# Nearest-neighbour upsampling: the input in two blocks of 61 and 451 rows per partition

## The chip, the core and the metric

The kernel runs on one core of one Trainium2 chip. The metric is the device time of one execution in microseconds; comparisons use the median of several runs.

## The reference

```python
batch, channels, h, w = x.shape          # 16, 64, 64, 64, float32
new_h, new_w = (h * scale_factor, w * scale_factor)      # scale_factor = 2
for i in range(new_h):
    for j in range(new_w):
        result[:, :, i, j] = x[:, :, i // scale_factor, j // scale_factor]
```

Each input row of 64 values becomes two equal output rows of 128 values, each value standing twice. The input has 16.78 MB, the output 67.11 MB.

## The kernel before

The input is seen as 65,536 rows of 64 floats (256 B). Partition p of 128 gets the 512 rows from 512 p on; their output is one stretch of 512 KB in HBM, 1 KB per input row. Everything lives in one SBUF tile, `mem`: ahead of the input area (`xt`, R = 512 rows) lies a free area of 79 output rows' size (`FREE`, `WF`).

Three loads, all issued by SP at L197, bring 32, 256 and 224 rows of each partition (`HEAD`, `cuts`). They are moved ahead of the program's opening barrier by `begin_before_barrier`.

Then nine steps follow, of the row counts in `rows`. In each, VectorE copies k input rows of every partition into an output buffer of k x 256 floats, reading each value twice and each row twice (`expanded`, L217; the first step's first row has a copy of its own at L216). Then one DMA stores the buffer (L219). Buffers alternate: even steps write at the front of the tile, odd steps just below the end of the input that has been consumed so far, so that the buffer grows into spent input. A step's copy therefore waits for the store two steps back, while the store one step back is under way. SP issues the stores of steps 0, 1 and 8, ACT the other six:

```python
rows = [54, 38, 54, 60, 54, 62, 64, 62, 64]
k0 = 1 if n == 0 else 0
issuer = nc.sync if n in (0, 1, len(rows) - 1) else nc.scalar
```

`close_early` rearranges the program's end so that only the last store's semaphore is waited for on SP after the closing barrier. Neither it nor `begin_before_barrier` is touched.

Of the kernel before, what the change touches and what calls it, by code (L numbers as in the profile page):

```python
# [153 lines left out]
@with_exitstack  # L154
def kernel(
    ctx: ExitStack,
    tc: tile.TileContext,
    x: bass.AP,
    scale_factor: int,
    out: bass.AP,  # L160
):
    nc = tc.nc
    nc.at_finalize(begin_before_barrier)
    nc.at_finalize(close_early)
    P = nc.NUM_PARTITIONS
    s = int(scale_factor)
    B, C, H, W = x.shape
    R = B * C * H // P
    fdt = x.dtype

    xp = x.rearrange("b c h w -> (b c h) w").rearrange("(p r) w -> p r w", p=P)
    op = out.rearrange("b c (h hd) w -> (b c h) (hd w)", hd=s).rearrange(
        "(p r) w -> p r w", p=P
    )

    rows = [54, 38, 54, 60, 54, 62, 64, 62, 64]
    GROW = s * s
    FREE = 79
    WF = FREE * GROW * W
    assert sum(rows) == R
    mem_pool = ctx.enter_context(tc.tile_pool(name="mem", bufs=1))
    LEAD = 32
    whole = mem_pool.tile([P, LEAD + WF + R * W], fdt, name="mem")
    mem = whole[:, LEAD:]
    xt = mem[:, WF:].rearrange("p (r w) -> p r w", r=R)  # L190

    HEAD = 32
    cuts = [0, HEAD, R // 2 + HEAD, R]
    for lo, hi in zip(cuts, cuts[1:]):
        nc.sync.dma_start(out=xt[:, lo:hi], in_=xp[:, lo:hi])  # L197

    def expanded(r0, r1):
        return (  # L200
            xt[:, r0:r1].unsqueeze(2).unsqueeze(4).to_broadcast([P, r1 - r0, s, W, s])
        )

    r0 = 0
    before = (0, 0)
    for n, k in enumerate(rows):
        size = k * GROW * W
        at = 0 if n % 2 == 0 else WF + r0 * W - size
        assert at >= before[1] or at + size <= before[0]
        before = (at, at + size)  # L210
        u = mem[:, at : at + size].rearrange(
            "p (k a w b) -> p k a w b", k=k, a=s, w=W
        )
        k0 = 1 if n == 0 else 0
        if k0:
            nc.vector.tensor_copy(out=u[:, :k0], in_=expanded(r0, r0 + k0))  # L216
        nc.vector.tensor_copy(out=u[:, k0:], in_=expanded(r0 + k0, r0 + k))  # L217
        issuer = nc.sync if n in (0, 1, len(rows) - 1) else nc.scalar
        issuer.dma_start(out=op[:, r0 : r0 + k, :], in_=u)  # L219
        r0 += k  # L220


# [33 lines left out]
```

## Time and profile before

| what | value |
|---|---|
| median of 3 runs | 197.28 us (197.05 to 197.37) |
| profiled execution, its own time | 197.08 us |
| its span, first to last instruction | 195.8 us |
| VectorE busy | 76.9 us in 10 copies |
| moved by DMA | 83.89 MB in 12 transfers, 1728 packets |
| mean rate over the span | 429 GB/s |

The span is what the profile shows; the time also holds what lies around it. A packet is one piece of a transfer on one of 16 DMA engines. "DMA" rows in the profile give the mean busy share of the 16 engines, "GB/s" what they moved, the bytes of a packet being booked as a whole, so that slices of a few microseconds scatter around the true rate.

### The profile page before, as it was taken

Reading aid. Unit: us, or ns where it says so; the run is one execution under the profiler, and the core shown is the slowest. Engines: PE = TensorE matmul, PEld = TensorE weight load, DVE = VectorE, ACT = ScalarE, POOL = GpSimd, SP = SyncE. Lnnn points to the kernel's source line nnn. Section 1 sums busy time; section 2 is a strip of 40 time slices with the busy share of each in tenths; the row PEclk is TensorE's granted clock in tenths of the full one; section 3 lists DMA queues with packets and bytes.
Section 4 is the critical chain, followed back from the end, with each engine's and each line's share of the span. In section 5 each row is a group of like instructions: output and inputs, shape, how many; then the busy total and the mean of one; then the engine's idle time right before and its main releaser. Section 6 shows DMA issues by size and latency. Waiting matters only on the chain.

```text
span 195.8 us, 76 instructions
## 1 busy us (share of the span) xinstructions
DVE 76.9 (39%) x10; POOL 0.2 (0%) x4
## 2 busy tenths in 40 slices
DVE  0000099990029287059008805920790079000000
POOL 0000000000000000000000000000000000000000
DMA  9999989989898988999999899999999999999994
GB/s 429 429 429 429 402 375 539 398 362 542 362 435 382 551 373 362 542 402 402 402 537 407 362 542 415 415 415 415 429 429 429 429 415 558 473 435 422 429 429 214
DMA packets 1728, 83.89 MB, mean 429 GB/s; under 512 B 192, under 2 KB 192, under 8 KB 192
## 3 DMA queue, kind: packets, MB, share of 16 engines
q10 hardware_dynamic: 864, 46.66, 55.0%
q1 hardware_dynamic: 864, 37.22, 44.2%
HBM read 16.78 MB, written 67.11 MB: 429 GB/s over the span
## 4 chain that ended last, share of the span: by engine, by line
DMA 61%; DVE 24%; SPq 0%; issue 0%
DMA out_dram<-mem 49%; DVE mem L217 24%; DMA mem<-in_x_dram 12%; SPq L197 0%
## 5 line engine op out<-in xcount | busy, mean ns | idle before, releaser
L217 DVE COPY mem<-mem 128x13824 f32<-128x13824 f32 (+5 forms) x9 | 76.6, 8515 | 84.6 <-DMA out_dram<-mem 65.6
L216 DVE COPY mem<-mem 128x256 f32<-128x256 f32 x1 | 0.3, 293 | 4.8 <-DMA mem<-in_x_dram 4.8
L237 POOL MEMSET const-bfloat16-1.0<- 128x1 bf16 x1 | 0.1, 102 | 0.0
L237 POOL MEMSET const-uint8-127<- 128x1 uint8 x1 | 0.1, 101 | 0.0
L237 POOL MEMSET const-float32-0.0<- 128x1 f32 x1 | 0.1, 98 | 0.2 <-issue 0.2
L237 POOL MEMSET const-float32-1.0<- 128x1 f32 x1 | 0.1, 98 | 0.0
## 6 DMA issues: line engine op xcount, KB each, us to landing
out_dram<-mem ACTq DMA_DIRECT2D x2, 7936.0 KB, 31.6
out_dram<-mem ACTq DMA_DIRECT2D x2, 6912.0 KB, 23.7
out_dram<-mem ACTq DMA_DIRECT2D x1, 7680.0 KB, 26.1
mem<-in_x_dram SPq DMA_DIRECT2D x1, 7168.0 KB, 40.2
out_dram<-mem SPq DMA_DIRECT2D x1, 6912.0 KB, 19.0
out_dram<-mem SPq DMA_DIRECT2D x1, 4864.0 KB, 25.2
mem<-in_x_dram SPq DMA_DIRECT2D x1, 1024.0 KB, 4.8
mem<-in_x_dram SPq DMA_DIRECT2D x1, 23.7
```

The costliest lines, as they stand in the source:

```text
L216: nc.vector.tensor_copy(out=u[:, :k0], in_=expanded(r0, r0 + k0))
L217: nc.vector.tensor_copy(out=u[:, k0:], in_=expanded(r0 + k0, r0 + k))
L237: nc = _bacc.Bacc("TRN2", target_bir_lowering=False, num_devices=1)
```

## The change

The rows of the input are cut into two blocks. Block A is the first 128 x 61 rows, 61 to a partition: in HBM it is one unbroken stretch, and so is its output. Block B is the rest, 451 rows to a partition. A is loaded first, in one DMA, into the last 61 rows of the SBUF input area; B follows in two loads of 227 and 224 rows. The steps go through B first and end with A as one step of 61 rows. The row counts of steps 5 to 8 become 64, 64, 63 and 61, and every step with an odd count gets a one-row copy ahead of an even one.

```diff
-    xp = x.rearrange("b c h w -> (b c h) w").rearrange("(p r) w -> p r w", p=P)
-    op = out.rearrange("b c (h hd) w -> (b c h) (hd w)", hd=s).rearrange(
-        "(p r) w -> p r w", p=P
-    )
-    rows = [54, 38, 54, 60, 54, 62, 64, 62, 64]
+    A = 61
+    N = P * A
+    xr = x.rearrange("b c h w -> (b c h) w")
+    outr = out.rearrange("b c (h hd) w -> (b c h) (hd w)", hd=s)
+    xa = xr[:N].rearrange("(p r) w -> p r w", p=P)
+    xb = xr[N:].rearrange("(p r) w -> p r w", p=P)
+    oa = outr[:N].rearrange("(p r) w -> p r w", p=P)
+    ob = outr[N:].rearrange("(p r) w -> p r w", p=P)
+    rows = [54, 38, 54, 60, 54, 64, 64, 63, A]
...
-    HEAD = 32
-    cuts = [0, HEAD, R // 2 + HEAD, R]
-    for lo, hi in zip(cuts, cuts[1:]):
-        nc.sync.dma_start(out=xt[:, lo:hi], in_=xp[:, lo:hi])
+    B0 = R - A
+    CUT = 227
+    nc.sync.dma_start(out=xt[:, B0:], in_=xa)
+    nc.sync.dma_start(out=xt[:, :CUT], in_=xb[:, :CUT])
+    nc.sync.dma_start(out=xt[:, CUT:B0], in_=xb[:, CUT:])
...
-        k0 = 1 if n == 0 else 0
+        k0 = 1 if n == 0 or k % 2 else 0
...
-        issuer.dma_start(out=op[:, r0 : r0 + k, :], in_=u)
+        dst = ob[:, r0 : r0 + k, :] if n < len(rows) - 1 else oa
+        issuer.dma_start(out=dst, in_=u)
```

## The prediction

> **What bounds the kernel now.** I read the page first: parts 1 to 3 for what is busy, then the chain, then the trace by windows and the DVE timeline.
>
> ```profile
> DVE 76.9 (39%) x10; POOL 0.2 (0%) x4
> ...
> DMA  9999989989898988999999899999999999999994
> ...
> DMA packets 1728, 83.89 MB, mean 429 GB/s; under 512 B 192, under 2 KB 192, under 8 KB 192
> ...
> HBM read 16.78 MB, written 67.11 MB: 429 GB/s over the span
> ```
>
> VectorE works for 76.9 of 195.8 us, while the 16 DMA engines are full in every slice but the last. The 192 packets under 512 B are the completions of 12 transfers on 16 engines; the other 1536 are one run per partition per transfer. So the time is 83.89 MB through 16 engines, plus whatever the engines lose at the two ends. The windows, cut by hand at the start and the end, show those losses.
>
> ```profile
> 0.00:1.00 1.00, 0.00 (x0) 0.20 (x4) 1.00 0.00 0
> 1.00:2.40 1.40, 0.00 (x0) 0.00 (x0) 1.00 0.97 252
> ...
> 40.00:190.00 150.00, 60.78 (x8) 0.00 (x0) 1.00 1.00 433
> 190.00:194.90 4.90, 0.00 (x0) 0.00 (x0) 1.00 0.99 428
> 194.90:195.80 0.90, 0.00 (x0) 0.00 (x0) 1.00 0.01 0
> ```
>
> The last two columns are the share of the DMA engines in use and GB/s. In the long middle the share is 1.00 at 433 GB/s. The sum of the span: 83.89 MB / 433 GB/s = 193.7 us; nothing moves in the first 1.0 us; from 1.0 to 2.4 us the engines are called busy (0.97) but move 252 instead of 433 GB/s, which loses 1.4 x (1 - 252/433) = 0.6 us. That makes 195.3, and the last 0.5 of 195.8 is the uneven finish of the engines and the last completions. Outside the span lie 1.3 us, since this execution took 197.08. The median of the three runs is 197.28, so the profiled run is 0.2 us on the low side; I work out a difference and put it on the median.
>
> So a change can gain only from the 1.0 + 0.6 + 0.5 us at the ends, unless it alters the 433. It can lose anywhere that a queue runs empty. The chain of waits must be read with that in mind:
>
> ```profile
> 0.43 23.65 DMA mem<-in_x_dram
> 24.09 0.02 issue
> 24.11 14.30 DVE mem L217
> 38.41 0.02 issue
> 38.42 19.01 DMA out_dram<-mem
> 57.44 0.02 issue
> 57.46 7.37 DVE mem L217
> 64.83 0.02 issue
> ```
>
> It gives 24% to DVE, but those are stretches with other transfers in flight beside them; the windows show no dip under them. The copies matter only if one of them outlasts the transfers queued ahead of its store.
>
> **The change part by part.**
>
> First, DMA work. Rows read and written are the same (61 + 451 = 512 per partition), and so are the three loads, the nine stores and the 128 runs in each. The first load doubles nearly, from 32 to 61 rows; the second shrinks from 256 to 227, so that both together are still 288 rows; the third stays at 224. Bytes and packets don't change: 0 us in the middle, if the rate holds at 433.
>
> Second, the addresses in HBM. Partitions of the input stand 512 x 256 B = 128 KiB apart before and 451 x 256 B = 112.75 KiB after; of the output 512 KiB before and 451 KiB after. Block A is one unbroken stretch: 61 rows next to 61 rows. No row shows the new distances. Loads and stores at the two old distances are alike. The load issues are
>
> ```profile
> L197 SPq DMA_DIRECT2D mem<-in_x_dram x3: 382/425/432, 0.0 to 0.9; - x3
> ...
> mem<-in_x_dram SPq DMA_DIRECT2D x1, 7168.0 KB, 40.2
> ```
>
> so the third load, issued at 0.9, landed near 41.1; 16.78 MB less the 0.35 MB of the ramp (252 GB/s for 1.4 us) from 2.4 to 41.1 is 425 GB/s, and 429 if the last 0.4 us is completion. Stores alone follow at 433. A fourfold distance makes no difference over about 1%, so I take 0 for the middle, with bounds of 1% to both sides (a rival each, below).
>
> The Trainium skill (DMA: Bandwidth & Descriptors, "Latency and other measured facts") has a row against large powers of two as row pitch: at 512 KiB 207 GB/s per direction, at a padded pitch 214. By that ratio the stores alone, 67.11 MB, would take some 5 us less after the change. The trace speaks against it: the stores at just that pitch run at 433 GB/s. The same page ("Where 436 GB/s comes from") puts the ceiling at 435 GB/s, by which the middle has under 1 us to give at any pitch; this speaks against the change, and the 433 agrees with it.
>
> Third, the ramp. The 0.6 us between 1.0 and 2.4 us is lost while 16 engines begin to read 8 KB runs from rows that stand 128 KiB apart. If it is address collision, the unbroken block removes it; if it is the time to the first data of any load, nothing changes. Bounds: -0.6 (all of it goes) and +0.3 (runs of 15.25 KB double the part of the ramp in which engines hold each other up, half of 0.6). No row tells the two apart. I take -0.15, a quarter of the loss, nearer to none since some latency must stay.
>
> Fourth, the first store. Before, the one-row copy of L216 ran while the second load was under way; now it waits for the second load, whose data it reads, and stands ahead of the 53-row copy.
>
> ```profile
> 4.83 0.29 DVE L216 COPY mem<-mem 128x256 f32<-128x256 f32 x1 [4.83 <-DMA mem<-in_x_dram]
> 24.11 19.55 DVE L217 COPY mem<-mem 128x13568 f32<-128x13568 f32 x2 [18.99 <-DMA mem<-in_x_dram]
> 38.42 5.60 SPq L219 DMA_DIRECT2D out_dram<-mem  x2
> ```
>
> 24.11 is the landing of 288 rows and stays. The 0.29 us (0.31 with the gap) moves onto the way to the first store: it is issued at 38.73 instead of 38.42. What hides it is the third load, landing at 41.1, its data over by perhaps 40.7. The first load needed 1.0 us from issue to data, so the store's data can flow from 39.7: hidden, and I take 0. If a store needs the whole ramp of the first load, 2.4 us, it is at full rate at 41.1, after the load's end: up to 0.4 us then. Both ends stay for the range. Queued behind that store on SP are only the second store and the last one; on DVE behind the one-row copy all others, none of them short of cover.
>
> Fifth, the other copies. The 63- and 61-row steps get a one-row copy ahead of an even one.
>
> ```profile
> L217 DVE COPY mem<-mem 128x16384 f32<-128x16384 f32 x2 | 17.4, 8694 | 18.6 <-DMA out_dram<-mem 18.6
> L217 DVE COPY mem<-mem 128x15872 f32<-128x15872 f32 x2 | 16.9, 8427 | 21.0 <-DMA out_dram<-mem 21.0
> L217 DVE COPY mem<-mem 128x13568 f32<-128x13568 f32 x1 | 14.3, 14286 | 19.0 <-DMA mem<-in_x_dram 19.0
> L217 DVE COPY mem<-mem 128x15360 f32<-128x15360 f32 x1 | 8.2, 8161 | 4.2 <-DMA out_dram<-mem 4.2
> ```
>
> The 53-row row shows why: an odd count cost 14.3 us where 54 to 64 rows cost 7.4 to 8.7. With the split, 63 rows cost 0.29 + 8.43 = 8.7 and 61 rows 0.29 + 8.16 = 8.5 us. Each copy waits for the store two back and is covered by the store one back, k rows of which take k x 131 KB / 433 GB/s = 0.303 k us: 19.4 us for 64 rows, 19.1 for 63. A margin of 10 us: 0. The thinnest later margin, the 4.2 us of the 60-row copy's wait after the 54-row one, sits in steps that don't change.
>
> Sixth, the last store: 61 rows instead of 64, one unbroken stretch, on the same SP queue, beside a 63-row store on ACT instead of a 62-row one. The end depends on the total per engine, which is the same. The 0.9 us of the last window without new data stays: 0, by at most 0.1 us either way.
>
> Sum: 0 - 0.15 + 0 + 0 + 0 = -0.15 us; the profiled execution would go from 197.08 to 196.9, the median from 197.28 to 197.1.
>
> **The rivals.** 0.2% of 197.28 is 0.4 us, about what a measurement of this kernel can tell from no change.
>
> *The ramp was collision* and goes, almost whole: -0.4 to -0.6, 196.7 to 196.9. For it speaks that engines were busy 0.97 at 252 GB/s; against it that the second and third load have the same distances and show no such loss. 0.18.
>
> *The power-of-two distance costs something all along.* If the 433 is held down by 1%, the bound from the load against the store rate, the stores gain 1.5 us: 195.8. Against it: a share of 1.00 at one steady rate, loads and stores alike. 0.04.
>
> *The first store comes late (slower).* Its place is the join of loads and stores near 41 us: issue at 38.73, and a queue that is dry from 40.7. It decides if a store takes over 2.0 us from issue to full rate; the price is up to 0.4 us, and with a ramp that is no better (or 0.1 to 0.3 worse) 197.7 to 198.0. Against it: the 1.0 us to first data, and descriptors that wait in the queue while the load drains. 0.12.
>
> *The new distances are the worse ones (slower).* At every second partition, loads now start on odd multiples of 256 B and stores on odd multiples of 1 KiB. A rate lower by 1% costs 1.9 us: 199.2. Against it: runs of 38 to 64 KB, for which a row's first bytes hardly count. 0.08.
>
> *The change does nothing to the ramp* is within the forecast.
>
> **How the numbers follow.** The forecast, within 0.4 us of 197.28 and likeliest 197.1, has 0.58. Faster: 0.18 + 0.04 = 0.22; slower: 0.12 + 0.08 = 0.20. The range takes in the vanished ramp below (197.28 - 0.6 = 196.7, less 0.1 for the end: 196.6) and the late first store above (197.28 + 0.4 = 197.7); outside are the two cases of another rate, 0.12, and half of 0.12 for a late store on top of a worse ramp.
>
> **What would show it.** The windows of the changed kernel: again 433 GB/s from 40 to 190 us (or another rate: the distances matter); 1.0 to 2.4 us above 252 GB/s if the ramp was collision, the same if it was latency. The one-row copy at 24.1, the first store at 38.7, and near 41 us a DMA share without a dip. DVE at some 77 us of busy time in 12 copies, none of over 9 us but the 53-row one. The forecast is wrong if the span leaves 195.4 to 196.2 us.

## The result and the profile after

| kernel | median of 8 runs | range |
|---|---|---|
| before | 197.25 us | 197.05 to 197.55 |
| changed | 197.83 us | 197.56 to 198.10 |

The ratio is 1.0028 (95% interval 1.0017 to 1.0039): slower by 0.6 us. The profiled execution took 197.56 us with a span of 196.2; before it was 197.08 and 195.8. So the changed kernel's profile shows 0.4 to 0.5 us of the loss.

The first three windows and the middle of the changed kernel, with the same cuts as before (share of the DMA engines and GB/s in the last two columns):

```profile
0.00:1.00 1.00, 0.00 (x0) 0.20 (x4) 1.00 0.00 0
1.00:2.40 1.40, 0.00 (x0) 0.00 (x0) 1.00 1.14 245
2.40:4.00 1.60, 0.00 (x0) 0.00 (x0) 1.00 0.89 381
...
40.00:190.00 150.00, 61.69 (x10) 0.00 (x0) 1.00 1.00 434
```

The middle is what it was, 434 for 433 GB/s. The start is not. A window of 2 us shows it best; here the line of before and then that of the changed kernel:

```profile
1.00:3.00 2.00, 0.00 (x0) 0.00 (x0) 1.00 0.99 307
```

```profile
1.00:3.00 2.00, 0.00 (x0) 0.00 (x0) 1.00 1.02 265
```

Windows this short book whole packets, so I size the loss by a landing instead. Both kernels bring 288 rows in their first two loads, 9.44 MB. The chain of waits of the changed kernel:

```profile
0.43 24.23 DMA mem<-in_x_dram
24.66 0.02 issue
24.68 0.29 DVE mem L221
24.98 14.21 DVE mem L222
39.19 0.02 issue
39.20 18.74 DMA out_dram<-mem
```

Those rows land at 24.66 us, 0.57 later than before (24.09). The third load, issued at 0.90, lands 40.7 us later:

```profile
mem<-in_x_dram SPq DMA_DIRECT2D x1, 7168.0 KB, 40.7
```

That is 41.6 instead of 41.1: 0.5 us behind, and so it stays to the end. What costs the time happens before 24.66 us; the join of loads and stores, the middle and the last store add nothing to it and win back at most 0.1 us.

A landing is that of the slowest of the 16 engines, and the packets in the traces show that the engines share the loss unequally. They begin the third load between 23.48 and 24.36 us (before: 23.37 to 23.78) and end it between 40.39 and 41.27 (40.31 to 40.76). So the first engine is about as early as before, the last one is 0.5 to 0.6 us later, and the time follows the last. At the join the faster engines do stand idle, 0.15 us each on average against 0.00 before, but the last one doesn't.

### The profile page after: what moved, and what is told of

The parts are those of the page before. It is cut to its first block, busy times and chain, and to the rows that moved or that the text cites. A ratio compares the mean times of both kernels' runs of the same rounds, so it can differ in the third digit from the quotient of the medians.

```text
span 196.2 us, 79 instructions
## 1 busy us (share of the span) xinstructions
DVE 77.0 (39%) x12; POOL 0.2 (0%) x4
## 3 DMA queue, kind: packets, MB, share of 16 engines
q1 hardware_dynamic: 864, 36.83, 43.8%
## 4 chain that ended last, share of the span: by engine, by line
DMA 61%; DVE 19%; DVEq 4%; SPq 0%; issue 0%
DMA out_dram<-mem 49%; DVE mem L222 19%; DMA mem<-in_x_dram 12%; DVEq L257 4%; DVE mem L221 0%; SPq L200 0%; DVEq L222 0%
## 5 line engine op out<-in xcount | busy, mean ns | idle before, releaser
L221 DVE COPY mem<-mem 128x256 f32<-128x256 f32 x3 | 0.9, 294 | 46.0 <-DMA mem<-in_x_dram 24.7
## 6 DMA issues: line engine op xcount, KB each, us to landing
mem<-in_x_dram SPq DMA_DIRECT2D x1, 7168.0 KB, 40.7
```

## The experiments

"Landing" below is the time at which 288 rows of every partition have landed, or would have landed: where the first loads bring fewer, the missing rows are added at 128 x 256 B / 433 GB/s = 0.0757 us each. Only such sums are compared. A run of so many KB is the stretch of HBM that a load reads for one partition, 128 of them to a load; the distance is that from one partition's run to the next. All times are medians, and the runs of before beside them gave 197.09 to 197.11 us.

| run | first load: rows, distance in HBM | time, us | ratio to before | landing, us |
|---|---|---|---|---|
| before | 32, 128 KiB | 197.25 | 1 | 24.09 |
| changed | 61, 15.25 KiB | 197.83 | 1.0028 (1.0017 to 1.0039) | 24.66 |
| e11, changed again | the same | 198.07 | 1.0046 (1.0032 to 1.0060) | 25.19 |
| e1 | 61, 128 KiB | 197.07 | 0.9998 (0.9989 to 1.0007) | 24.05 |
| e2 | 32, 15.25 KiB | 199.22 | 1.0109 (1.0095 to 1.0122) | 24.84 |
| e3 | 227, 112.75 KiB | 198.24 | 1.0065 (1.0051 to 1.0079) | 24.45 |
| e4 | 16, 128 KiB | 198.09 | 1.0051 (1.0038 to 1.0063) | 24.07 |
| e5 | 64, 16 KiB | 197.54 | 1.0024 (1.0013 to 1.0035) | 24.58 |
| e6 | 61, 112.75 KiB | 197.31 | 1.0006 (0.9998 to 1.0015) | 24.20 |
| e7 | 61, 15.25 KiB | 199.23 | 1.0107 (1.0092 to 1.0123) | 25.17 |
| e8 | 61, 64 KiB | 197.14 | 1.0003 (0.9994 to 1.0012) | 24.20 |
| e9 | 61, 15.25 KiB | 197.69 | 1.0028 (1.0017 to 1.0040) | 24.83 |
| e10 | 61, 32 KiB | 197.15 | 1.0002 (0.9994 to 1.0011) | 24.30 |

**Run length or address.** The first load differs from that of before in two things: its runs are 15.25 KB long instead of 8, and its rows lie next to each other instead of 128 KiB apart. e1 keeps the first and undoes the second:

```diff
-    xa = xr[:N].rearrange("(p r) w -> p r w", p=P)
-    xb = xr[N:].rearrange("(p r) w -> p r w", p=P)
+    xp = xr.rearrange("(p r) w -> p r w", p=P)
...
+    xa = xp[:, R - A :]
+    xb = xp[:, : R - A]
...
```

(and the output alike).

> The changed kernel, but its block of 61 is the last 61 rows of every partition's 512, so that all distances in HBM are those of before (128 KiB in, 512 KiB out); sizes, order, SBUF places and copies are those of the changed kernel. Theory 1 (the loss lies in the first microseconds and comes from the longer runs, 15.25 KB, of the first load): 288 rows land at 24.7 us as in the changed kernel, time 197.8. Theory 2 (the loss comes from the closeness of the unbroken block's addresses): 288 rows at 24.1, time 197.25. Theory 3 (the new distances slow the whole): 197.25 with a middle as before.

It ran as before did. Its landing of 288 rows and its windows:

```profile
0.42 23.63 DMA mem<-in_x_dram
```

```profile
1.00:3.00 2.00, 0.00 (x0) 0.00 (x0) 1.00 1.02 312
...
40.00:190.00 150.00, 61.09 (x10) 0.00 (x0) 1.00 1.00 434
```

This one run clears everything but the addresses: the longer first load, the new steps and copies, the order in SBUF, and the later first store, which it issues at 38.59 us and which costs nothing. Theory 1 falls. e2 does the reverse, 8 KB runs from rows 15.25 KiB apart:

```diff
-    nc.sync.dma_start(out=xt[:, B0:], in_=xa)
+    nc.sync.dma_start(out=xt[:, B0 : B0 + 32], in_=xa[:, :32])
...
+    nc.sync.dma_start(out=xt[:, B0 + 32 :], in_=xa[:, 32:])
```

> The changed kernel, but the first load brings only 32 of the block's 61 rows (8 KB runs, rows still 15.25 KB apart); the other 29 are a fourth load behind the rest. Theory 1 (long runs): the ramp is that of before, time 197.3. Theory 2 (close addresses): the ramp stays bad, time 197.8. Theory 3: 197.8.

```profile
0.43 22.22 DMA mem<-in_x_dram
```

```profile
1.00:3.00 2.00, 0.00 (x0) 0.00 (x0) 1.00 0.99 225
```

259 rows land at 22.65 us (0.43 + 22.22), which makes 24.84 for 288: the start is as bad as the changed kernel's, or worse, with the old run length. So gaps between the rows don't help either. The run was far slower than any theory had expected, and lost over 1 us more later on; for that see the early store below.

e4 changes the run length alone, on the kernel before:

```diff
-    HEAD = 32
+    HEAD = 16
```

> The kernel before with a first load of 16 rows (4 KB runs) instead of 32; the third load takes the 16 rows more. Theory 1 (long runs): a better ramp than before, by some 0.2 to 0.3 us: 197.0. Theories 2 and 3: as before, 197.25.

272 rows land at 22.86, which makes 24.07 for 288: with runs of 4, 8 and 15.25 KB at 128 KiB the start is the same within 0.04 us. Yet the run was 1.0 us slower, which no theory had expected. The third load says where:

```profile
mem<-in_x_dram SPq DMA_DIRECT2D x1, 7680.0 KB, 41.4
```

Issued at 0.9, it lands at 42.3 instead of 41.1. Something delays the end of the loads, and the first store is issued at 37.20 here, 1.2 us earlier than before. e3 exchanged the first two loads, so its first store came still earlier, at 34.37:

```diff
-    nc.sync.dma_start(out=xt[:, B0:], in_=xa)
     nc.sync.dma_start(out=xt[:, :CUT], in_=xb[:, :CUT])
+    nc.sync.dma_start(out=xt[:, B0:], in_=xa)
```

> The changed kernel with its first two loads exchanged: the 227 rows (56.75 KB runs, rows 112.75 KiB apart) come first, the unbroken block second; the first copy starts earlier, at some 20 us. Theory 1 (long runs): the ramp gets worse still, 198.5 or more if the loss grows with the run. Theory 2 (close addresses): it is as good as before, 197.3 or less. Theory 3: 197.8.

Its 198.24 us looks like theory 1, but isn't: 0.36 us of the 1.1 lie in the landing, the rest again at the end of the third load (issued at 0.90, landing 41.3 us later at 42.2). These two needed a control.

**The store that comes early.** e7 takes away the slow copy that holds the first store back:

```diff
-        k0 = 1 if n == 0 or k % 2 else 0
+        k0 = 1 if k % 2 else 0
```

> The changed kernel without the one-row copy in the first step: 54 rows in one copy of 7.4 us, so that the first store is issued at 32.1 us instead of 39.2. Theory J (a store that waits in the queue while the third load ends holds that load's last runs up; it is what made the runs with 4 KB runs and with the rest first slow): the third load's landing moves by 1.2 us, time 199.0. Rival (an early store only waits in its queue and costs nothing): 197.8.

```profile
25.20 7.37 DVE mem L222
32.57 0.02 issue
32.59 27.58 DMA out_dram<-mem
```

```profile
mem<-in_x_dram SPq DMA_DIRECT2D x1, 7168.0 KB, 42.9
```

The store is issued 6.6 us earlier than in the changed kernel, and the third load lands at 43.8 instead of 41.6; 0.5 of the 2.2 us is a worse start in that execution (25.17 for 24.66). The time is 1.2 to 1.4 us above the changed kernel's two medians (198.07 and 197.83). So a store that comes early delays the end of the loads, and the 14.3 us copy of 53 rows in both kernels, which looks like waste, earns its keep by issuing the store late.

The packets in the traces show where. In e3, e4 and e7 it is the last stretch of the third load that each of the 16 engines reads, and hardly another: 2.4 to 3.8 us for stretches that otherwise take 2.1 (2.3 in e4). The engines begin these last ones between 38.2 and 39.7 us. The kernel before issues its store at 38.42 us, when the first of them are under way, and they keep their 2.1 to 2.2 us. e4, e3 and e7 issue it 1.0, 4.0 and 5.7 us ahead of the first of them, and they take 1.0, 0.8 and 1.0 us longer on average. So what counts here is whether the store is queued some time before the last stretches begin, not how long it waits. It would account for the late third loads of e3 (0.7 us after its start is taken off) and e4 (1.2 us), and e2 fits (store at 37.19 us, loads landing until 43.0, though there the fourth load has close rows too); only e7 tests it directly. The starts of these runs are read from the landing alone.

**Which distance.** e5 gives the unbroken block 64 rows, so that distances are 16 and 112 KiB:

```diff
-    A = 61
+    A = 64
...
-    CUT = 227
+    CUT = 224
```

> The changed kernel with an unbroken block of 64 rows (rows 16 KiB apart in the input) and a rest of 448 (112 KiB apart); steps 54, 38, 54, 60, 54, 62, 62, 64, 64, no odd ones. Theory 2a (closeness: the first reads of the 16 engines all fall into 2 MB of HBM): 288 rows land at 24.7 us, time 197.8. Theory 2b (distances that are no power of two are the bad ones): 24.1, time 197.2.

e6 keeps the changed kernel's layout with its odd distances, but loads 61 rows of the rest first and the unbroken block second:

```diff
+    nc.sync.dma_start(out=xt[:, CUT - A : CUT], in_=xb[:, CUT - A : CUT])
     nc.sync.dma_start(out=xt[:, B0:], in_=xa)
-    nc.sync.dma_start(out=xt[:, :CUT], in_=xb[:, :CUT])
+    nc.sync.dma_start(out=xt[:, : CUT - A], in_=xb[:, : CUT - A])
     nc.sync.dma_start(out=xt[:, CUT:B0], in_=xb[:, CUT:])
```

> The changed kernel, its input brought in another order: first 61 rows of the rest (same size and runs as the block, but 112.75 KiB apart), then the unbroken block, then the 166 rows that make up 288, then the last 224. The first copy waits for the third load, so that the first store is issued at the same point. Theory 2a (closeness): 112.75 KiB is as far as 128, 288 rows land at 24.1, time 197.25, and the block costs nothing as second load. Theory 2b (no power of two): 24.4 or more, time 197.6 to 197.8.

Four loads come ahead of the steps here, so `EARLY`, the number of loads that are moved ahead of the opening barrier, is 4 instead of 3; so it is in e8 and e10. The landing and the window of e5, then those of e6:

```profile
0.42 24.16 DMA mem<-in_x_dram
```

```profile
1.00:3.00 2.00, 0.00 (x0) 0.00 (x0) 1.00 1.06 262
```

```profile
0.89 23.30 DMA mem<-in_x_dram
```

```profile
1.00:3.00 2.00, 0.00 (x0) 0.00 (x0) 1.00 1.03 305
3.00:5.00 2.00, 0.00 (x0) 0.00 (x0) 1.00 1.04 445
```

The 288 rows land at 24.58 and at 24.20 us. A neat power of two is about as bad as 15.25 KiB, and the odd 112.75 KiB is good: closeness, not oddness. e6 is the changed kernel repaired by the order of its loads alone. The block, read as the second load, costs nothing that the time shows. At 197.31 us e6 doesn't beat before either.

e8 and e10 fill in distances of 64 and 32 KiB by other blocks (256 + 256 and 128 + 384 rows); e9 takes the unbroken block from the input's end; e11 is the changed kernel run again. In e8 `xa` and `xb` are the halves of S = 256 rows per partition, and A is still 61. Its loads:

```diff
-    nc.sync.dma_start(out=xt[:, B0:], in_=xa)
-    nc.sync.dma_start(out=xt[:, :CUT], in_=xb[:, :CUT])
-    nc.sync.dma_start(out=xt[:, CUT:B0], in_=xb[:, CUT:])
+    nc.sync.dma_start(out=xt[:, S - A : S], in_=xa[:, S - A :])
+    nc.sync.dma_start(out=xt[:, S : S + 32], in_=xb[:, :32])
+    nc.sync.dma_start(out=xt[:, : S - A], in_=xa[:, : S - A])
+    nc.sync.dma_start(out=xt[:, S + 32 :], in_=xb[:, 32:])
```

e10, block and loads:

```diff
-    A = 61
+    A = 128
...
-    CUT = 227
-    nc.sync.dma_start(out=xt[:, B0:], in_=xa)
+    CUT = 160
+    nc.sync.dma_start(out=xt[:, B0 : B0 + 61], in_=xa[:, :61])
+    nc.sync.dma_start(out=xt[:, B0 + 61 :], in_=xa[:, 61:])
     nc.sync.dma_start(out=xt[:, :CUT], in_=xb[:, :CUT])
     nc.sync.dma_start(out=xt[:, CUT:B0], in_=xb[:, CUT:])
```

e9 (the output alike):

```diff
-    N = P * A
+    N = P * (R - A)
...
-    xa = xr[:N].rearrange("(p r) w -> p r w", p=P)
-    xb = xr[N:].rearrange("(p r) w -> p r w", p=P)
+    xa = xr[N:].rearrange("(p r) w -> p r w", p=P)
+    xb = xr[:N].rearrange("(p r) w -> p r w", p=P)
```

What was expected of e8, e10, e9 and e11, in this order:

> The input in two halves of 256 rows per partition (64 KiB apart in the input, 256 KiB in the output), steps 54, 38, 54, 60, 50, 64, 64, 64, 64; first load the last 61 rows of the first half, then 32 rows of the second, then the first half's other 195, then the rest; first store issued at the same point. Theory 2a: between near and far, 288 rows at 24.1 to 24.7, time 197.25 to 197.8. Theory 2b: as before, 24.1 and 197.25.

> Two blocks of 128 and 384 rows per partition (32 and 96 KiB apart in the input); first load 61 of the 128 rows, then the other 67, then 160 of the rest, then the last 224; steps 54, 38, 54, 60, 54, 62, 62, 64, 64. The first reads fall into 4 MB instead of 2 (15.25 to 16 KiB apart) or 8 (64 KiB apart). Theory 2a: where between the two the loss begins; 288 rows between 24.2 and 24.7, time 197.2 to 197.7. Its rival, that only a block without gaps is bad, is spoken against by the run with 8 KB runs; it expects 24.2 and 197.2 here.

> The changed kernel with the unbroken block of 61 taken from the end of the input instead of its beginning; all else the same. Theory 2a (closeness of the addresses, wherever they lie): as the changed kernel, 288 rows at 24.6 to 24.7 us, time 197.7. Theory 2c (it is the first 2 MB of the input that are slow to begin with): 24.1, 197.2.

> The changed kernel, unaltered, beside the two others on the same chip: 197.7, 288 rows at 24.6 to 24.7 us, if the loss belongs to the kernel and not to one execution.

The windows of e8, e10, e9 and e11, in this order:

```profile
1.00:3.00 2.00, 0.00 (x0) 0.00 (x0) 1.00 1.11 359
```

```profile
1.00:3.00 2.00, 0.00 (x0) 0.00 (x0) 1.00 1.06 297
```

```profile
1.00:3.00 2.00, 0.00 (x0) 0.00 (x0) 1.00 1.03 258
```

```profile
1.00:3.00 2.00, 0.00 (x0) 0.00 (x0) 1.00 1.09 258
```

The landings of e10 and e9:

```profile
0.89 23.40 DMA mem<-in_x_dram
```

```profile
0.42 24.41 DMA mem<-in_x_dram
```

In these runs the window has 297 GB/s or more from 32 KiB on, and the time is that of before; at 16 KiB and below it has 265 or less, at the input's beginning and at its end. So the loss belongs to closeness, and it becomes clear between 32 and 16 KiB, that is where the 128 runs of the first load lie within 2 MB of HBM rather than 4. Whether it is the distance or the whole stretch that counts, no run tells, since all have 128 runs. e11 shows how the changed kernel scatters: the same code landed 288 rows 0.5 us later than in its first profile, and later than expected. It is one engine that makes most of the difference: it ended its part of the third load at 41.79 us, the next at 41.10. On the same chip e9 took 197.57 to 197.84 us and e11 197.89 to 198.17, so the block's place may matter a little too.

Open: what makes close addresses slow in the first few microseconds only; why an early store holds the last load up; and the 0.25 us by which e3's landing (227 rows of 56.75 KB runs first) is later than e6's at the same distance.

## Why the prediction was wrong

The bound of the kernel, the sum of the span and the places where a change could act were right: bytes at 433 GB/s, and a loss that could only sit at the ends.

The failed step is the third, the ramp. I took -0.15 us between bounds of -0.6 and +0.3; it measured +0.57 in the profile (landing 24.66 for 24.09) and the median rose by 0.58, outside both the bound and the range (197.83 for at most 197.7). Two things were wrong in it. The sign: I let an unbroken block remove address collisions, from the thought that rows at a power of two collide; e1, e5 and e6 show that far rows start well whether odd or even, and close ones badly. And the upper bound: I took it from the run length, which e4 and e1 show to have no effect from 4 to 15.25 KB, so it bounded the wrong cause. The trace of before had no row for close addresses, and then the loss of 0.6 could as well have doubled, which would have been a bound of +0.6.

The second step, 0 for the middle, held: 434 GB/s at the new distances, 433 and 434 (e1) at the old. The Trainium skill's row against a pitch of 512 KiB, measured on copies between HBM tensors and with its 214 GB/s at a padded 4 MiB pitch (DMA: Bandwidth & Descriptors, "Latency and other measured facts"), therefore doesn't reach these stores from SBUF, while its ceiling of 435 GB/s (same page, "Where 436 GB/s comes from") agrees with these rates.

The fourth step, 0 for a store issued 0.3 us later, held (e1, at 38.59 us). Its rival, a store that comes late, shows only as the 0.15 us that the faster engines of the changed kernel stood idle, with the store issued at 39.20; what costs time is a store that comes early, 1.2 to 1.4 us for 6.6 us (e7), and no rival had that. The fifth and sixth, 0 for the copies and the last store, held: e1 has the copies and a last store of 61 rows and runs as before, and in the changed kernel nothing more is lost behind the landing. Of the slower rivals, the one on distances had the right word and the wrong mechanism: it feared odd distances and a lower rate all along, and the runs show close ones and a worse first load.

## What to carry to other kernels

In a kernel that keeps its DMA engines full, look for the loss where they start, and size it by the landing of a fixed number of bytes, which is that of the slowest engine, not by short windows, which are averages. Give the first load addresses that lie far apart (here 32 KiB or more between partitions) and put a compact block second, where it cost nothing here. Before speeding up a copy that releases the first store, see whether its slowness keeps that store out of the loads' way.

## What had not been expected of the hardware

A first load whose 128 runs lie within 2 MB starts worse than one whose runs are spread over 4 MB or more: 225 to 265 GB/s against 297 to 359 in the window from 1 to 3 us (first loads of 32 to 64 rows), and 288 rows land 0.3 to 1.1 us later. As the second load the same block cost nothing (e6). A store queued 1.0 us or more before the engines began the last stretches of the last load moved that load's landing by 1.2 us (e4) and, with the start taken off, by 0.7 (e3) and 1.7 us (e7); one queued at 38.42 us, as the engines began them, did not (before).
